# RWKV mixer: the decay's and the rate's narrow projections placed between the key tiles, the values' lerp and the gate behind them

## The chip, the cores and the metric

The kernel runs on one core of a Trainium2 chip. TensorE (PE in the profile) multiplies matrices into PSUM, VectorE (DVE), ScalarE (ACT) and GpSimd (POOL) do the elementwise work, and SyncE (SP) issues most of the transfers. Each engine takes its instructions strictly in its own order, and waits where one needs something that another engine or a transfer has not delivered. The metric is device time in microseconds for one execution, the median of the runs shown. Lower is better.

## The reference

Two layers over 512 latent and 256 context tokens of width 1024. Layer 0 is attention with a feed-forward network, layer 1 is bidirectional RWKV-7 time mixing with a feed-forward network; a last norm gives the output. The change lies in the branches of the time mixer:

```python
def _rwkv_branches(u, mix, w_rkv, w0, w1, w2, a0, a1, a2, g1, g2, k_k, k_a, readout):
    xx = _centred_shift_delta(u)          # 0.5 * (left + right neighbour) - u

    def lerp(j):
        return u + xx * mix[j]

    sel = (0, 2, 3) if readout else (2, 3)
    proj = jnp.einsum('jbtd,jde->jbte', jnp.stack([lerp(s) for s in sel]), w_rkv[-len(sel):])
    k = proj[-2].astype(jnp.float32)
    kk = heads(k * k_k)
    kk = kk * lax.rsqrt(jnp.maximum(jnp.sum(kk * kk, axis=-1, keepdims=True), 1e-24))
    xw, xa = lerp(1), lerp(4)
    for d in range(2):
        w_log = -jax.nn.softplus(-(w0[d] + jnp.tanh(xw @ w1[d]) @ w2[d])) - 0.5
        decay = jnp.exp(-jnp.exp(w_log))
        a = jax.nn.sigmoid(a0[d] + (xa @ a1[d]) @ a2[d])
        k_d = k * (1.0 + (a - 1.0) * k_a)
    r = heads(proj[0])
    g = (jax.nn.sigmoid(lerp(5) @ g1) @ g2)
    return r, heads(proj[-1]), kk, dirs, g
```

So there are six lerps of the same input u and its shift xx. Three feed wide projections (1024 to 1024: r, keys, values), three feed narrow ones (1024 to 128: the decay's w1 of both directions, the rate's a1 of both directions, the gate's g1). A scan over the tokens per direction then uses all of them.

## The kernel before

Activations lie feature-major: 8 tiles (index k or f) of 128 features by 768 tokens (512 for what only the latent tokens need). Every product is made of three matmuls in a reduced 32-bit format: high part times high part, high times low, low times high. A cast on ACT gives the high part of a tile, a subtraction on DVE or POOL the low part. So each lerp tile costs a multiply-add on DVE (`lt`, L911), a cast on ACT (`lh`, L913) and a subtraction (`ll`, L915) of which two in three go to POOL and the others to DVE; each block of weights costs casts on ACT (L218) and subtractions on DVE (L219).

The order in program text of the stage is this. Layer 0 ends with feed-forward products (L445), whose sums are added to xT (L258); both streams are then normed (L521, L522). `dense` (L921) makes the keys: the shift on POOL (L886), the keys' lerp (in its first form, per stream), four weight blocks of 256 columns, two key tiles each; `sink_k` (L948) copies the sums to `kt` (L950) and stores them, squares them (L953) and sums the squares by head on PE (L955, `ssk`). A loop (L972) then makes the decay (w1), the gate (g1) and the rate (a1): a lerp of all eight tiles, its weights, 24 or 48 matmuls. The root of the keys' norm follows (L994 to L1005, `rsy`, `rn`), then the eight normed keys (L1006 to L1014): load `kt`, spread the norm over the features on PE (L1011), multiply (`kkt`, L1013), store. Then come the values' lerp (L1015) and r's lerp (L1018), which is stored to memory and projected later (`project_r`, PE `pr`, L1357).

Behind that scope come the values' products (PE `pv`, L1239 to L1241, 576 matmuls of 256 columns), the elementwise tiles of the scan (`elem`; its first products are `z`, L1073), the triangular inversion on DVE (`invert`, L1169 to L1193), and the scan.

The scheduler orders the instructions of each engine; the text and the pools decide what it may do. Two rules of the pools matter. Tiles with one tag in one pool share a fixed number of buffers, so a new tile waits for the last reader of an older one; lerps share `lt` (two buffers) and a ring of 13 slots for `lh` and `ll`, eight in pool `lp` and five in `lp2`. And pools are stacked from both ends of the memory, so a pool opened later uses the room of one that has been closed and waits for its last readers. On the right stand `lp`, then `lp2`, then the weights' pool `wpj`; when their scope ends, the values open a weights' pool of their own behind `lp`. The scan's tiles (`Xs`, L1040 and others) lie in the room of xT, xx and the other tiles of the key stage on the left.

Of the kernel before, what the change touches and what calls it, by code (L numbers as in the profile page):

```python
# [10 lines left out]
F32 = mybir.dt.float32  # L11
# [26 lines left out]
def tile_hybrid_backbone(ctx: ExitStack, tc: tile.TileContext, a: dict, out: bass.AP, dbg=None, stop=None, start=None):  # L38
# [812 lines left out]
    with ExitStack() as rw:  # L851
# [9 lines left out]
        with ExitStack() as de:  # L861
            lp2 = pool(de, "lp2", side="right")
            wp = pool(de, "wpj", side="right")
# [14 lines left out]
            pk = pool(de, "pk", 1, psum=True)  # L878

# [8 lines left out]
            slots = {"n": 0, "l": 0}  # L888
# [32 lines left out]
            def dense(j, row, n, sink, first=False):  # L921
                xh, xl = lerp(j, n, first=first)
                for b in range(4):
# [7 lines left out]
                    for q in range(2):  # L931
                        if not (first and b == 0):
                            products(items[q:q + 1], xh, xl, KT)
                        out_ = sink(2 * b + q, ps[q][1])
                    if first and b == 0:
# [12 lines left out]
            def sink_k(f, ps):  # L948
                t = ep.tile([P, T], F32, name="kt", tag="kt")
                nc.vector.tensor_copy(t, ps)  # L950
# [7 lines left out]
            dense(2, 1, T, sink_k, True)  # L958
# [13 lines left out]
            for j, nm_, n, dst, fn in ((1, "rwkv_w1", T, t1, AF.Tanh), (5, "rwkv_g1", L, None, AF.Sigmoid),  # L972
                                       (4, "rwkv_a1", T, ta, AF.Copy)):
                xh, xl = lerp(j, n)
                wh, wl = (wp.tile([P, KT, P], F32R, name=z, tag="wd" + z[1], bufs=2) for z in ("wh", "wl"))
                for k0 in range(0, KT, 4):
                    raw = wp.tile([P, 4, P], F32, name="wraw", tag="wdr", bufs=2)
                    if nm_ == "rwkv_g1":
                        nc.sync.dma_start(out=raw, in_=a[nm_][0].rearrange("(k p) f -> p k f", p=P)[:, k0:k0 + 4])
                    else:  # L980
                        for d in range(2):
                            nc.sync.dma_start(out=raw[:, :, 64 * d:64 * d + 64],
                                              in_=a[nm_][0, d].rearrange("(k p) f -> p k f", p=P)[:, k0:k0 + 4])
                    nc.scalar.copy(wh[:, k0:k0 + 4], raw)
                    nc.vector.tensor_tensor(out=wl[:, k0:k0 + 4], in0=raw, in1=wh[:, k0:k0 + 4], op=ALU.subtract)
                outs, full = proj_psum(n)
                product(outs, lambda k: wh[:, k, :], lambda k: wl[:, k, :], xh, xl, KT)
# [530 lines left out]
```

## Time and profile before

| | us |
|---|---|
| median of 3 runs | 2232.61 (2231.56 to 2236.65) |
| profiled execution | 2237.59 |
| its span | 2235.8 |

Busy time of the engines over the span, as the page gives it:

| engine | busy us | share |
|---|---|---|
| PE (matmul) | 2006.4 | 90% |
| DVE | 1636.2 | 73% |
| ACT | 1136.6 | 51% |
| POOL | 693.1 | 31% |

The profile is of one execution. A row of the timeline has the start, the time, the engine, the line, the operation, what it writes and reads, and, in brackets, how long the engine stood idle before it and what ended that. A row of groups has the count, the busy time, the mean of one in ns, and the idle time before them. A row of windows has the length of the stretch, then for PE, PE's weight loads, DVE, ACT and POOL the busy time and the count, then the mean granted clock of PE, the share of the DMA engines and the rate.

### The profile page before, as it was taken

What the parts mean: (1) busy time and instruction counts of PE and PEld (TensorE: products, weight loads), DVE (VectorE), ACT (ScalarE), POOL (GpSimd) and SP (SyncE); (2) the same over time, 40 slices, a digit from 0 to 9 for tenths busy, and PEclk for the clock granted to TensorE, in tenths of its full rate; (3) what the DMA queues carried; (4) which work ended last, traced back from release to release, by engine and by line L of the source; (5) the groups of instructions that cost most, each with busy time, mean ns of one, the idle gap of its engine ahead of it and who ended that gap; (6) DMA issues with size and microseconds to landing.
All of it is one profiled execution on the core that took longest, in us unless ns stands there. A gap on an engine that the chain in (4) does not pass through costs nothing.

```text
span 2235.8 us, 43048 instructions
## 1 busy us (share of the span) xinstructions
PE 2006.4 (90%) x16566; PEld 1770.4 (79%) x16566; DVE 1636.2 (73%) x3105; ACT 1136.6 (51%) x2326; POOL 693.1 (31%) x572
## 2 busy tenths in 40 slices
PE   6998999898999999996988978776988687999998
PEld 4995555697999999995867956665777586899998
DVE  4565555768777777767565598699575778999997
ACT  6436556655333333336343765766665556444443
POOL 1120000126445444423132231221110416666661
PEclk8999999998999999997988989887889888999999
DMA  7206663353221222221336674774645654333332
GB/s 269 99 16 226 227 228 111 122 162 132 76 76 57 76 64 78 66 62 62 102 107 201 181 215 144 216 207 133 188 120 166 185 156 139 117 105 95 104 97 74
DMA packets 249708, 294.12 MB, mean 132 GB/s; under 512 B 36216, under 2 KB 176736, under 8 KB 248992
## 3 DMA queue, kind: packets, MB, share of 16 engines
q1 hardware_dynamic: 248144, 288.42, 41.6%
q8 instruction: 131, 2.15, 0.4%
q0 software_dynamic: 1008, 2.36, 0.3%
q10 hardware_dynamic: 352, 0.60, 0.1%
q14 instruction: 73, 0.60, 0.1%
HBM read 228.40 MB, written 50.33 MB: 125 GB/s over the span
## 4 chain that ended last, share of the span: by engine, by line
PE 65%; DVE 14%; DMA 7%; ACT 6%; issue 5%; POOL 3%; SPq 1%; DVEq 0%; POOLq 0%; ACTq 0%
PE yps L445 12%; PE A L395 8%; PE C L395 5%; PE B L395 5%; PE yps L228 5%; PE po L786 3%; PE pj L228 3%; PE S L767 2%; PE PTp L781 2%; PE mps L126 2%; PE qps L634 2%; PE qps L636 2%; PE qps L635 2%; DVE wu L241 2%; DMA wr<-in_ffn_wu_dram 2%
## 5 line engine op out<-in xcount | busy, mean ns | idle before, releaser
L445 PE MATMUL yps<-gh,wu 128*128 128x384 f32 (+2 forms) x1120 | 323.6, 344 | 0.2 <-DVE xT L258 0.2
L258 DVE SCALAR_TENSOR_TENSOR xT<-yps,modT,xT 128x384 f32<-128x384 f32 (+3 forms) x360 | 185.3, 537 | 119.7 <-PE yps L445 102.1
L239 ACT CAST wu<-wr 128x512 fp32r<-128x512 f32 x276 | 168.5, 619 | 170.6 <-PE A L395 56.4
L239 ACT CAST wu<-ws 128x512 fp32r<-128x512 f32 x176 | 109.2, 621 | 223.8 <-PE yps L445 65.9
L445 PEld LDWEIGHTS yps<-gh,wu 128*128 128x128 f32 x1120 | 202.6, 189 | 11.6 <-DVE xT L258 0.4
L241 POOL TENSOR_TENSOR wu<-wr,wu 128x512 fp32r<-128x512 f32 x86 | 124.8, 1451 | 232.1 <-ACT wu L239 198.4
L445 PE MATMUL yps<-gl,wu 128*128 128x384 f32 (+2 forms) x560 | 192.5, 344 | 0.0
L349 POOL TENSOR_TENSOR ws<-wr 128x512 f32<-128x512 f32 x88 | 130.2, 1484 | 146.0 <-DMA wr<-in_ffn_wg_dram 68.6
L241 DVE TENSOR_TENSOR wu<-wr,wu 128x512 fp32r<-128x512 f32 x190 | 164.3, 869 | 13.4 <-ACT wu L239 12.9
L241 DVE TENSOR_TENSOR wu<-ws,wu 128x512 fp32r<-128x512 f32 x111 | 137.7, 1241 | 21.9 <-ACT wu L239 21.8
L241 POOL TENSOR_TENSOR wu<-ws,wu 128x512 fp32r<-128x512 f32 x65 | 98.9, 1523 | 64.7 <-ACT wu L239 64.6
L228 PE MATMUL yps<-oTh,wu 128*128 128x384 f32 (+1 forms) x512 | 111.3, 309 | 1.1 <-ACT wu L239 1.0
L445 PEld LDWEIGHTS yps<-gl,wu 128*128 128x128 f32 x560 | 105.9, 189 | 4.3
L770 DVE TENSOR_REDUCE mx<-S 128x1 f32<-128x768 f32 (+1 forms) x96 | 74.7, 778 | 44.9 <-PE S L767 44.3
L1156 POOL TENSOR_SCALAR_AFFINE_SELECT GA<-GA 64x512 f32<-64x512 f32 x48 | 41.1, 857 | 202.6 <-ACT GA L1154 191.9
L395 PE MATMUL C<-x5h,wu 128*128 128x384 f32 (+1 forms) x352 | 86.4, 323 | 14.4 <-ACT x5h L312 12.3
L782 ACT COPY PT<-PTp 128x384 f32<-128x384 f32 (+1 forms) x160 | 69.3, 465 | 53.9 <-PE PTp L781 53.8
L781 PEld LDWEIGHTS PTp<-ident,pr 128*128 128x128 f32 x448 | 50.2, 144 | 50.5 <-issue 23.6
L228 PEld LDWEIGHTS yps<-oTh,wu 128*128 128x128 f32 x512 | 85.3, 188 | 1.9 <-ACT wu L239 1.4
L395 PE MATMUL B<-x2h,wu 128*128 128x384 f32 (+1 forms) x352 | 84.7, 309 | 1.3 <-POOL wu L241 1.2
L395 PE MATMUL A<-x1h,wu 128*128 128x384 f32 (+1 forms) x352 | 82.5, 310 | 3.3 <-POOL wu L241 1.7
L241 POOL TENSOR_TENSOR wu<-mw,wu 128x512 fp32r<-128x512 f32 x2 | 2.9, 1446 | 264.6 <-ACT wu L239 264.6
(411 smaller groups left out, 6328.7 us busy)
## 6 DMA issues: line engine op xcount, KB each, us to landing
mw<-in_mod_w_dram SPq DMA_DIRECT2D x48, 1024.0 KB, 5.4
wr<-in_ffn_wg_dram SPq DMA_DIRECT2D x44, 512.0 KB, 4.0
wr<-in_ffn_wu_dram SPq DMA_DIRECT2D x44, 512.0 KB, 3.9
wr<-in_ffn_wd_dram SPq DMA_DIRECT2D x44, 512.0 KB, 3.9
d_b<-BK SPq DMA_DIRECT2D x24, 512.0 KB, 4.3
Bs<-d_b SPq DMA_DIRECT2D x48, 256.0 KB, 3.7
wraw<-in_rwkv_wrkv_dram SPq DMA_DIRECT2D x32, 256.0 KB, 3.2
wr<-in_rwkv_wo_dram SPq DMA_DIRECT2D x16, 512.0 KB, 4.2
```

Of the source, the lines that this page charges most:

```text
L126: nc.tensor.matmul(ps[32 * g:32 * g + 32, :], sc[:, k, :], w[:, k - nk * i, :], start=(k < 4), stop=(k >= 4))
L228: nc.tensor.matmul(ps, w(k), x(k, sl), start=(k == 0 and i == 0), stop=(k == nk - 1 and i == 2))
L239: nc.scalar.copy(hi, raw)
L241: (nc.gpsimd if lane["n"] % 3 == 0 else nc.vector).tensor_tensor(out=lo, in0=raw, in1=hi, op=ALU.subtract)
L258: nc.vector.scalar_tensor_tensor(out=xT[:, f, t0:t1], in0=ps[:, t0 - sl.start:t1 - sl.start], scalar=modT[:, l, 8 * m + f, s:s + 1], in1=x ...
L349: nc.gpsimd.tensor_tensor(out=t, in0=x, in1=y, op=op)
L395: nc.tensor.matmul(ps, w[:, k], x[:, k], start=(k + j == 0), stop=(k == 3 and j == 2))
L445: nc.tensor.matmul(ps, u[k // 2][w][:, k % 2, fs], gs[k // 2][x][:, k % 2, sl], start=(k + j == 0), stop=(k == nk - 1 and j == 2))
L770: nc.vector.tensor_reduce(out=mx, in_=S[:, :nk * P], axis=AX.X, op=ALU.max)
L781: nc.tensor.transpose(ps[:, t - t0, :], pr_[:, P * t:P * t + P], ident)
L782: nc.scalar.copy(PT[h][:, t0:t1, P * qt:P * qt + P], ps[:, :t1 - t0, :])
L786: nc.tensor.matmul(po[HD * h:HD * h + HD, :], vt[:, k0 // P + t, HD * kv:HD * kv + HD], PT[h][:, t, :], start=(t == 0), stop=(t == nk - 1))
```

## The change

Five things change, all in the key stage.

1. The weights' pool `wpj` is opened ahead of `lp2`, so it stands directly behind `lp` and the ring's five slots lie further in. The values' own weights' pool, opened later behind `lp`, then has the place of the old one.
2. The decay and the rate become generators (`low_rank`) with their own weight tiles (`wl_p`), their own PSUM tile of two banks (`pl`), and lerp tiles from the five slots of `lp2`. `dense` calls them behind a key tile: one half of the decay (four of the eight lerp tiles and their 24 matmuls) behind the fourth key tile and one behind the sixth, and the halves of the rate behind the seventh and the eighth.
3. `kt` is copied by ACT instead of DVE.
4. The root of the norm, two normed keys, the values' lerp, six normed keys, the gate, r's lerp: that is the order behind the keys. The gate was ahead of the rate and of the norm.
5. The loop that made the three narrow projections is gone.

```diff
         with ExitStack() as de:
+            wp = pool(de, "wpj", side="right")
             lp2 = pool(de, "lp2", side="right")
-            wp = pool(de, "wpj", side="right")
...
             pk = pool(de, "pk", 1, psum=True)
+            pl = pool(de, "pl", 1, psum=True)
+            wl_p = pool(de, "wlr")
...
                         out_ = sink(2 * b + q, ps[q][1])
+                        if between:
+                            between(b, q)
...
-                nc.vector.tensor_copy(t, ps)
+                nc.scalar.copy(t, ps)
...
+            def low_rank(j, nm_, n, dst, fn, runs):
+                wh, wl = (wl_p.tile([P, KT, P], F32R, name=z, tag=z) for z in ("wh", "wl"))
+                for k0 in range(0, KT, 4):
+                    raw = wp.tile([P, 4, P], F32, name="wraw", tag="wdr", bufs=2)
...
+                    nc.scalar.copy(wh[:, k0:k0 + 4], raw)
+                    nc.vector.tensor_tensor(out=wl[:, k0:k0 + 4], in0=raw, in1=wh[:, k0:k0 + 4], op=ALU.subtract)
+                ps = pl.tile([P, 1024], F32, name="lr", tag="lr")
+                outs = [(ps[:, off:off + w], slice(off, off + w)) for _, off, w in STREAMS if off < n]
+                for run in runs:
+                    for k in run:
+                        hi, lo = (lp2.tile([P, n], F32R, name=z, tag=f"{z}{8 + slots['r'] % 5}") for z in ("lh", "ll"))
+                        slots["r"] += 1
+                        lerp_part(j, k, hi, lo, slice(0, n))
+                        for i, (w, x) in enumerate(((wh, hi), (wh, lo), (wl, hi))):
+                            for o, sl in outs:
+                                nc.tensor.matmul(o, w[:, k], x[:, sl], start=(k == 0 and i == 0), stop=(k == KT - 1 and i == 2))
+                    if run[-1] < KT - 1:
+                        yield
+                if dst is None:
+                    dst = ep.tile([P, T], F32, name="tg", tag="kt")[:, :n]
+                    nc.scalar.activation(dst, ps[:, :n], fn)
+                    nc.sync.dma_start(out=d_g, in_=dst)
+                else:
+                    nc.scalar.activation(dst, ps[:, :n], fn)
+
+            two = [range(0, 4), range(4, KT)]
+            factors = {(1, 1): low_rank(1, "rwkv_w1", T, t1, AF.Tanh, two), (3, 0): low_rank(4, "rwkv_a1", T, ta, AF.Copy, two)}
+            factors[2, 1], factors[3, 1] = factors[1, 1], factors[3, 0]
+            dense(2, 1, T, sink_k, True, lambda b, q: next(factors.get((b, q), iter(())), None))
...
-            for j, nm_, n, dst, fn in ((1, "rwkv_w1", T, t1, AF.Tanh), (5, "rwkv_g1", L, None, AF.Sigmoid),
-                                       (4, "rwkv_a1", T, ta, AF.Copy)):
-                xh, xl = lerp(j, n)
...
-            for f in range(KT):
+            def normed_keys(f):
...
+            for f in range(2):
+                normed_keys(f)
             vxh, vxl = lerp(3, T, lp)
+            for f in range(2, KT):
+                normed_keys(f)
+            for _ in low_rank(5, "rwkv_g1", L, None, AF.Sigmoid, [range(KT)]):
+                pass
```

The scheduler turns this into new orders. In the changed kernel line numbers behind L877 are higher by 2 to 23; names say what is what. Three places follow.

First, DVE at the end of layer 0, where xT takes the last feed-forward sums (`yps`) and the squares of the norm are summed (`acc`). Before, no weight block of the keys is split there:

```order
L241 TENSOR_TENSOR wu<-wr,wu 128x512
L385 TENSOR_TENSOR gl<-gt,gh 128x384
L258 SCALAR_TENSOR_TENSOR xT<-yps,modT,xT 128x256 x3
L178 TENSOR_TENSOR acc<-acc,sq 128x256 x2
L258 SCALAR_TENSOR_TENSOR xT<-yps,modT,xT 128x256
L178 TENSOR_TENSOR acc<-acc,sq 128x256
L258 SCALAR_TENSOR_TENSOR xT<-yps,modT,xT 128x512
```

The same place in the changed kernel:

```order
L241 TENSOR_TENSOR wu<-wr,wu 128x512
L385 TENSOR_TENSOR gl<-gt,gh 128x384
L219 TENSOR_TENSOR wlo<-wraw,whi 128x512
L258 SCALAR_TENSOR_TENSOR xT<-yps,modT,xT 128x256
L219 TENSOR_TENSOR wlo<-wraw,whi 128x512
L258 SCALAR_TENSOR_TENSOR xT<-yps,modT,xT 128x256 x2
L178 TENSOR_TENSOR acc<-acc,sq 128x256
L258 SCALAR_TENSOR_TENSOR xT<-yps,modT,xT 128x256
L178 TENSOR_TENSOR acc<-acc,sq 128x256
L219 TENSOR_TENSOR wlo<-wraw,whi 128x512
```

All eight subtractions of the first two blocks (`wlo`), with their casts on ACT, now stand among these; before, they stood between the norm and the keys' lerp.

Second, PE behind the fourth key tile. Its last products and, behind them, what is new (`lr` is the narrow projection's sum; the rows go on like this to 24):

```order
L228 MATMUL pj<-lh,wlo 128x512
L228 MATMUL pj<-lh,wlo 128x256
L984 MATMUL lr<-lh,wh 128x512
L984 MATMUL lr<-lh,wh 128x256
L984 MATMUL lr<-ll,wh 128x512
L984 MATMUL lr<-ll,wh 128x256
L984 MATMUL lr<-lh,wl 128x512
L984 MATMUL lr<-lh,wl 128x256
```

Before, the next key tile's products followed there, and the decay's products came behind all keys. There are four such pieces now, and the values' products begin behind the last normed key as before. Of these, 238 stood ahead of the first z before, and 153 stand there now; between the first z and the end of the fourth elementwise tile there are nearly as many as before (317 and 313), and behind that tile 110 instead of 21.

Third, DVE between the keys and the values' products. Before, these are lerps of the rate, the first of the values, and normed keys (`kkt`):

```order
L1013 SCALAR_TENSOR_TENSOR kkt<-kt,hkk,pj 128x768
L911 SCALAR_TENSOR_TENSOR lt<-xx,par_78,xT 128x768 x2
L1013 SCALAR_TENSOR_TENSOR kkt<-kt,hkk,pj 128x768
L915 TENSOR_TENSOR ll<-lt,lh 128x768
L911 SCALAR_TENSOR_TENSOR lt<-xx,par_78,xT 128x768 x2
L1013 SCALAR_TENSOR_TENSOR kkt<-kt,hkk,pj 128x768 x2
L911 SCALAR_TENSOR_TENSOR lt<-xx,par_78,xT 128x768
L219 TENSOR_TENSOR wlo<-wraw,whi 128x512 x2
L911 SCALAR_TENSOR_TENSOR lt<-xx,par_78,xT 128x768
```

In the changed kernel the values' lerps are over at this place, and between the normed keys stand the last lerps of the gate (512 wide) and r's (L1041, which is L1018 before):

```order
L1030 SCALAR_TENSOR_TENSOR kkt<-kt,hkk,pj 128x768
L913 SCALAR_TENSOR_TENSOR lt<-xx,par_78,xT 128x512
L917 TENSOR_TENSOR ll<-lt,lh 128x512
L913 SCALAR_TENSOR_TENSOR lt<-xx,par_78,xT 128x512 x2
L1030 SCALAR_TENSOR_TENSOR kkt<-kt,hkk,pj 128x768
L1041 SCALAR_TENSOR_TENSOR lt<-xx,par_78,xT 128x512
L917 TENSOR_TENSOR ll<-lt,lh 128x512
L1030 SCALAR_TENSOR_TENSOR kkt<-kt,hkk,pj 128x768
L1041 SCALAR_TENSOR_TENSOR lt<-xx,par_78,xT 128x512
L1030 SCALAR_TENSOR_TENSOR kkt<-kt,hkk,pj 128x768
```

The weights of the values' first two blocks (eight `wlo`) are split ahead of the third normed key; before, the first of them stood behind the last.

More of the change, by code (lines that the diff above doesn't have):

```diff
@@ L886, in shift @@
                 nc.gpsimd.tensor_tensor(out=y[:, 1:w - 1], in0=x[:, 0:w - 2], in1=x[:, 2:w], op=ALU.add)
-            slots = {"n": 0, "l": 0}
+            slots = {"n": 0, "l": 0, "r": 0}
             def lerp(j, n, own=None, first=False):
@@ L919, in proj_psum, with dense @@
                 return [(ps[:, off:off + w], slice(off, off + w)) for _, off, w in STREAMS if off < n], ps[:, :n]
-            def dense(j, row, n, sink, first=False):
+            def dense(j, row, n, sink, first=False, between=None):
                 xh, xl = lerp(j, n, first=first)
@@ L956, in sink_k @@
                 return t
-            dense(2, 1, T, sink_k, True)
+            def low_rank(j, nm_, n, dst, fn, runs):
+                wh, wl = (wl_p.tile([P, KT, P], F32R, name=z, tag=z) for z in ("wh", "wl"))
+                for k0 in range(0, KT, 4):
+                    raw = wp.tile([P, 4, P], F32, name="wraw", tag="wdr", bufs=2)
+                    if nm_ == "rwkv_g1":
+                        nc.sync.dma_start(out=raw, in_=a[nm_][0].rearrange("(k p) f -> p k f", p=P)[:, k0:k0 + 4])
+                    else:
+                        for d in range(2):
+                            nc.sync.dma_start(out=raw[:, :, 64 * d:64 * d + 64],
+                                              in_=a[nm_][0, d].rearrange("(k p) f -> p k f", p=P)[:, k0:k0 + 4])
+                    nc.scalar.copy(wh[:, k0:k0 + 4], raw)
[16 more added lines that the diff above has]
+                    nc.sync.dma_start(out=d_g, in_=dst)
+                else:
+                    nc.scalar.activation(dst, ps[:, :n], fn)
@@ L971, in tile_hybrid_backbone @@
             nc.vector.tensor_copy(hsel, ps)
-            for j, nm_, n, dst, fn in ((1, "rwkv_w1", T, t1, AF.Tanh), (5, "rwkv_g1", L, None, AF.Sigmoid),
-                                       (4, "rwkv_a1", T, ta, AF.Copy)):
-                xh, xl = lerp(j, n)
[L975 to L987, printed above, removed]
-                if dst is None:
-                    dst = ep.tile([P, T], F32, name="tg", tag="kt")[:, :n]
-                    nc.scalar.activation(dst, full, fn)
-                    nc.sync.dma_start(out=d_g, in_=dst)
-                else:
-                    nc.scalar.activation(dst, full, fn)
             sm_, y_, t_ = (nm.tile([P, 6 * NH], F32, name=z) for z in ("ssm", "rsy", "rst"))
```

## The prediction

> **What bounds the kernel now.** I read the page first, for the span and the chain that ended last.
>
> ```profile
> span 2235.8 us, 43048 instructions
> PE 65%; DVE 14%; DMA 7%; ACT 6%; issue 5%; POOL 3%; SPq 1%; DVEq 0%; POOLq 0%; ACTq 0%
> ```
>
> PE (TensorE) has two thirds of the chain, but that is a mean over many stages. So I cut the stretch that the change touches, the key part of the RWKV mixer and what follows it, into windows at events named below: from the end of layer 0 to the first key tiles, the other six key tiles, the narrow projections and the normed keys, the values up to the first decay product (`z`), and two more up to the end of the projection of r.
>
> ```profile
> core 0: us, PE busy (x) PEld busy (x) DVE busy (x) ACT busy (x) POOL busy (x), PEclk, DMA share, GB/s
> 1023.00:1070.00 47.00, 27.91 (x124) 23.51 (x123) 39.83 (x66) 32.27 (x63) 17.62 (x26) 0.71 0.16 55
> 1070.00:1132.00 62.00, 60.15 (x375) 53.59 (x374) 30.64 (x36) 18.08 (x25) 9.26 (x5) 1.00 0.32 103
> 1132.00:1184.00 52.00, 41.61 (x165) 29.52 (x164) 44.30 (x47) 23.91 (x34) 21.88 (x14) 0.78 0.50 158
> 1184.00:1222.00 38.00, 32.94 (x239) 31.73 (x240) 23.24 (x27) 13.37 (x25) 10.13 (x9) 0.90 0.60 197
> 1222.00:1281.00 59.00, 58.82 (x504) 56.78 (x503) 28.06 (x50) 39.80 (x94) 11.96 (x19) 0.97 0.60 166
> 1281.00:1384.00 103.00, 84.89 (x742) 64.97 (x743) 95.10 (x210) 59.35 (x135) 27.11 (x32) 0.90 0.64 187
> ```
>
> The second row is PE's alone: 60.2 of 62 us, at a granted clock of 1.00, with DVE (VectorE) half idle and POOL (GpSimd) almost so. The third is the reverse: DVE 44.3 of 52 us, PE at clock 0.78. The fifth is PE's again, the last DVE's (95.1 of 103). The change shifts work from the third window into the second. The timeline has the events:
>
> ```profile
> 1042.81 0.79 PE L228 MATMUL pj<-lh,whi 128*128 128x256 f32 x2 [8.40 <-ACT lh L913]
> 1132.30 1.04 PE L970 MATMUL hps<-ident,hb 128*48 128x128 f32 x8
> 1184.55 1.01 PE L1239 MATMUL pv<-whi,lh 128*128 128x256 f32 x3 [3.71 <-ACT whi L218]
> 1186.78 0.58 PE L1240 MATMUL pv<-wlo,lh 128*128 128x256 f32 x1 [1.22 <-DVE wlo L219]
> 1213.20 1.82 POOL L1040 MEMSET Xs<- 128x2048 f32 x1 [18.44 <-DVE lt L1018]
> 1221.73 0.67 PE L1073 MATMUL z<-t,wa 128*128 128x256 f32 x2 [3.05 <-DMA wa<-in_rwkv_w_dram]
> 1280.70 1.99 DVE L1169 STREAM_TRANSPOSE E<-AB 128x1024 f32<-128x1024 f32 x1 [4.41 <-ACT AB L1161]
> 1281.06 0.28 PE L1240 MATMUL pv<-wlo,lh 128*128 128x256 f32 x1
> 1281.18 0.28 PE L1241 MATMUL pv<-whi,ll 128*128 128x256 f32 x1
> 1298.06 0.79 PE L1357 MATMUL pr<-rh,whi 128*128 128x512 f32 x1 [0.26 <-ACT whi L218]
> 1383.48 0.39 PE L1357 MATMUL pr<-rh,wlo 128*128 128x512 f32 x1
> ```
>
> Keys end at 1132.3, values (`pv`) run from 1184.6 to 1281.3, the first z stands at 1221.7 because its tiles overlay xx and xT, which L1018 on DVE reads last. The triangular inversion starts at 1280.7.
>
> **Part 1, weights ahead of the norm.** Of the first two weight blocks, eight casts on ACT and eight subtractions on DVE move into the tail of layer 0, as the first pair of order listings shows.
>
> ```profile
> L219 DVE TENSOR_TENSOR wlo<-wraw,whi 128x512 fp32r<-128x512 f32 x8 | 6.0, 752 | 1.0 <-ACT whi L218 0.8
> L218 ACT CAST whi<-wraw 128x512 fp32r<-128x512 f32 x8 | 4.9, 612 | 3.4 <-DMA wraw<-in_rwkv_wrkv_dram 3.4
> 1043.72 0.69 DVE L219 TENSOR_TENSOR wlo<-wraw,whi 128x512 fp32r<-128x512 f32 x1 [0.17 <-ACT whi L218]
> 1044.73 0.69 DVE L219 TENSOR_TENSOR wlo<-wraw,whi 128x512 fp32r<-128x512 f32 x1
> ```
>
> Not all 6.0 us lie on the path. I count one subtraction ahead of the norm's second half (0.7), the two inside the lerps (1.4), and two casts between the modulations (1.2): **3.3 us** earlier for the first key tiles. The ends are 0 (the region is no earlier free) and 6.0. Its cover is layer 0's tail, where PE is full and DVE waits for PE; without cover the same 6.0 come back there. Two subtractions of the decay's own factor take the place of two that left before the norm's second half; I don't count them.
>
> **Part 2, decay and rate among the keys.** On PE nothing is added or taken away; 96 matmuls move.
>
> ```profile
> 1100.45 8.44 PE pj L228 x48
> 1108.89 1.23 PE ssk L955 x12
> ```
>
> ```profile
> L911 DVE SCALAR_TENSOR_TENSOR lt<-xx,par,xT 128x768 f32<-128x768 f32 x12 | 15.2, 1286 | 1.7 <-POOL ll L915 1.7
> L1013 DVE SCALAR_TENSOR_TENSOR kkt<-kt,hkk,pj 128x768 f32<-128x768 f32 x8 | 8.1, 1011 | 2.9 <-DMA kt<-d_k 1.7 <-PE pj L1011 1.1
> L915 POOL TENSOR_TENSOR ll<-lt,lh 128x768 fp32r<-128x768 f32 x8 | 15.2, 1907 | 17.4 <-ACT lh L913 17.4
> ```
>
> The first two rows are the chain of waits within the second window, the others groups of the third, each with its count, busy time, mean in ns and idle time before it. One key tile is 48 matmuls in 8.44 us, so each half of a narrow projection (24 of the same shapes) is 4.2 us. Three halves stand ahead of the last key tile's end, one behind it. Keys then end at 1132.3 - 3.3 + 12.7 = **1141.7**, PE full as now. That needs sixteen lerps in time, each 1.3 us of DVE and for two in three 1.9 of POOL, where that window has 31 and 53 us idle; a late one makes PE wait in order, 1.9 us at each of four places. I take none. The copy of `kt` goes from DVE to ACT: eight at no more than the 1.0 of a kkt, which reads PSUM too, beside PE on either engine (ACT has 44 us idle there). If a tile's sums came free too late for the next but one, PE would wait that 1.0 at each; I take nothing.
>
> **Part 3, what is left behind the keys.** Now values' lerps, gate and normed keys stand between the keys and the values' products, and DVE does them in order (third pair of listings). Its prices, with the window's own contention in them, are those groups and these:
>
> ```profile
> L911 DVE SCALAR_TENSOR_TENSOR lt<-xx,par,xT 128x512 f32<-128x512 f32 x8 | 7.9, 998 | 0.0
> L915 DVE TENSOR_TENSOR ll<-lt,lh 128x768 fp32r<-128x768 f32 x5 | 5.3, 1068 | 0.0
> L985 DVE TENSOR_TENSOR wl<-wraw,wh 128x512 fp32r<-128x512 f32 x4 | 2.7, 684 | 0.2 <-ACT wh L984 0.2
> L915 DVE TENSOR_TENSOR ll<-lt,lh 128x512 fp32r<-128x512 f32 x2 | 1.7, 853 | 0.0
> L915 POOL TENSOR_TENSOR ll<-lt,lh 128x512 fp32r<-128x512 f32 x6 | 8.0, 1344 | 14.2 <-ACT lh L913 14.2
> L1000 DVE SCALAR_TENSOR_TENSOR rsy<-rst,rsy 128x96 f32<-128x96 f32 x1 | 1.3, 1282 | 0.0
> L971 DVE CAST hsel<-hps 48x1024 fp32r<-48x1024 f32 x1 | 1.2, 1209 | 0.0
> 1159.41 1.82 POOL L915 TENSOR_TENSOR ll<-lt,lh 128x768 fp32r<-128x768 f32 x1 [0.52 <-ACT lh L913]
> 1159.61 2.43 DVE L911 SCALAR_TENSOR_TENSOR lt<-xx,par,xT 128x768 f32<-128x768 f32 x1
> 1163.01 1.01 DVE L911 SCALAR_TENSOR_TENSOR lt<-xx,par,xT 128x768 f32<-128x768 f32 x1
> ```
>
> The last key product needs a PSUM slot that the sixth `kkt` frees, and values follow it in PE's order. Up to that `kkt` DVE has: seven of the values' lerps 9.0 (their slots come free with the last key tile), two of their subtractions 2.1, eight gate lerps 8.0 and three subtractions 2.6, six kkt 6.1, ten weight subtractions 6.8 (two of the gate's factor, eight of the values' blocks, which used to come behind), hsel and rsy 2.5, and five short ones on the way to the norm with the first r lerp, for which I estimate 3.5 at the 0.7 of a weight subtraction. Sum 40.6. The idle time in it is bounded below by none, above by the 7.7 that stands before DVE now (52.0 - 44.3). Without contention (1.01 instead of 1.286, and as much off the narrower ones) it is 4 us less. So 37 to 48; I take **42**, near the rows' own sum: little of the idle time stays, as the first two key tiles are loaded early. (On SP's queue eight loads of values' weights now stand ahead of the third; if it comes late, that is the 1.7 of kkt's row, within the 7.7.) Values' products start at 1141.7 + 42 = **1183.7**, against 1184.6: almost all that was won is spent behind the keys, since DVE's work there is as long as before, only with other contents. Two more waits are new: the first values' PSUM bank is that of the gate's sum, so PE also waits for the sigmoid behind a table load on ACT; with the last gate product ahead of the last kkt this is covered, uncovered it is the load and the sigmoid, of which I have no row here and which I bound by the 3.7 that pv waits for ACT now. PE's clock is low in the block either way (0.78 now), so values start slowly as they do now.
>
> **Part 4, behind the start of the values.** Here the order gains more.
>
> ```profile
> L1018 DVE SCALAR_TENSOR_TENSOR lt<-xx,par,xT 128x512 f32<-128x512 f32 x8 | 5.9, 747 | 4.3 <-DMA d_rl<-lt 4.3
> ```
>
> The lerps are done, both first weight blocks loaded (3.7 and 1.2 us of waits in the rows above go, of which the start already holds the first), and L1018's eight reads of xx stand directly behind the normed keys. The first z follows 153 values' products instead of 238. At 0.12 us each (the two rows at 1281) that is 10.2 us less, with 1.2 + 3.1 of waits gone: 1183.7 + 37.2 - 10.2 - 4.3 = 1206.4, that is **15.3 earlier**. Its tiles allow it if the last read of xx is over by about 1197.9 (now 8.5 us lie between them): two kkt and seven reads fill 7.3 us behind the start, with the 4.3 that they wait for transfers 11.6: at 1195.3 they are over. The inversion starts 15.3 earlier too, as PE's order between z and it holds the same work. But the 85 products come behind z: values end at 1281.3 - 15.3 + 10.2, **5.1 earlier**. The projection of r can't start before that (its tiles lie where the values' lerps lay), and the next elementwise tiles live where r's lay. So the gain at 1383.5 lies between 5.1 (r follows the values) and 15.3 (DVE full, all of its lead kept). I take **8**, nearer to the first, as PE has 85 of 103 us there. Behind it nothing is changed and I carry the 8 us through.
>
> **Sum.** The profiled execution took 2237.59 us, its span 2235.8; it would take 2229.6. The median shown, 2232.61, lies 5 below that execution; less the same 8 us it gives **2224.6**.
>
> **Rivals.**
> *All of DVE's lead is kept*: r's projection is fed sooner as well, and the 18 us in which PE is idle after 1281 shrink. For it: DVE 92% busy there. Against: r's start. Gain 15 to 16, 2217.
> *Spent twice*: the block behind the keys takes 48 instead of 42. Values start at 1189.7 and end at 1282.2, so r is 1 later, the inversion 9 earlier: 2232, no change.
> *The port, slower*: while POOL subtracts, DVE's lerp took 2.43 instead of 1.01 (the two rows above; POOL's began at 1159.41). Ten such subtractions now fall into the block, five at 1.9 and five at 1.3, 16.3 us. If DVE stood for all of each, on 37 + 7.7, the block takes 61, values start 18 later and end 13 later: 2246. It decides from a block of 47 us on, where the values' end is no longer earlier. Against it: now fourteen such operations cost about 5 us, not 23.2.
> The Trainium skill, SBUF — State Buffer, "Who interferes with whom", says that a DVE instruction with two SBUF inputs and a GpSimd instruction that reads SBUF exclude each other for the whole instruction. By that rule the time would be this rival's; the trace agrees in the row of 2.43 us, and disagrees in its mean of 1.286 us.
> *Not what it says*: the weights' region is free no earlier, and part 1 is 0: 2228.
>
> **How the numbers follow.** Forecast 0.40, all kept 0.22, spent twice 0.18, port 0.12, region 0.08. What a measurement can tell from no change is about 0.2%, 4.5 us. Faster: 0.36 of the forecast, 0.22, 0.02 and 0.05 of the others, 0.65. Same: 0.04, 0.13 and 0.03, 0.20. Slower: 0.15. The range reaches to the first rival and past no change, with the block at 37 to 48 in it (6 us each way): 2213 to 2236; the port lies outside.
>
> **What would show it.** Part 1: the first pj after layer 0 about 2 us earlier, no weight casts between the modulations. Part 2: PE full between the key tiles, `hps` at about 1146. Part 3: first pv at 1178 to 1190, DVE over 85% busy before it. Part 4: first z at 1206, values' end at 1276, inversion at 1265, r's end at 1375. I am wrong if PE waits for `ll` among the keys, if pv starts before 1175 or after 1190, or if r's end doesn't move though the inversion does.

## The result: 0.7% slower, and the profile after

| | us |
|---|---|
| changed kernel, median of 13 runs | 2253.55 (2247.23 to 2258.35) |
| kernel before, median of 13 runs beside them | 2236.72 (2231.56 to 2251.51) |
| ratio, 95% interval | 1.0068 (1.0054 to 1.0082) |
| profiled execution, its span | 2256.64, 2254.9 |

By the ratio that is about 15 us more, where 8 less were forecast. The page's first line and its chain of waits read much as they did:

```profile
span 2254.9 us, 43054 instructions
PE 65%; DVE 14%; DMA 8%; ACT 5%; issue 4%; POOL 3%; SPq 1%; DVEq 0%; POOLq 0%; ACTq 0%
```

So the difference has to be looked for at events. First the clock of the comparison must be set right. The last product of layer 0, in the timeline of before and then of after:

```profile
1022.94 0.40 PE L445 MATMUL yps<-gh,wu 128*128 128x512 f32 x1
```

```profile
1027.96 0.40 PE L445 MATMUL yps<-gh,wu 128*128 128x512 f32 x1
1045.59 0.58 PE L228 MATMUL pj<-lh,whi 128*128 128x256 f32 x1 [6.96 <-ACT lh L915]
1147.96 0.51 PE L228 MATMUL pj<-lh,whi 128*128 128x512 f32 x2
1167.69 0.37 PE L1020 MATMUL rnp<-ident,rsy 128*16 128x128 f32 x1 [12.24 <-DVE rsy L1017]
1200.01 0.58 PE L1262 MATMUL pv<-whi,lh 128*128 128x256 f32 x1 [5.25 <-ACT tg L989]
1220.39 0.38 PE L1096 MATMUL z<-t,wa 128*128 128x256 f32 x1
1279.08 2.04 DVE L1192 STREAM_TRANSPOSE E<-AB 128x1024 f32<-128x1024 f32 x1 [4.41 <-ACT AB L1184]
1290.24 0.28 PE L1264 MATMUL pv<-whi,ll 128*128 128x256 f32 x1
1357.30 2.03 DVE L1192 STREAM_TRANSPOSE E<-AB 128x1024 f32<-128x1024 f32 x1 [2.33 <-ACT AB L1184]
1396.64 0.39 PE L1380 MATMUL pr<-rh,wlo 128*128 128x512 f32 x1
```

The 5.0 us at layer 0's end are not shown to be the change's: PE's order is the same in both kernels up to the third key tile, over the fourteen executions profiled for this study that product stands anywhere from 1019.8 to 1028.0, and e9 below, in which PE, DVE, ACT and POOL have the changed kernel's order up to there and far beyond, reaches it at 1022.8. So all that follows is counted in us behind it. The inversions are numbered from (0) in order of time. "Last key product" is the last one of two high parts (`lh,whi`); four more, 0.7 us, end the keys.

| event | before | forecast | after |
|---|---|---|---|
| first key product | 19.9 | 16.6 | 17.6 |
| last key product | 108.5 | 117.9 | 120.2 |
| first product of the values | 161.6 | 160.8 | 172.0 |
| first z | 198.8 | 183.5 | 192.4 |
| inversion (0) | 257.8 | 242.5 | 251.1 |
| last product of the values | 258.2 | 253.1 | 262.3 |
| inversion (1) | 319.8 | | 329.3 |
| last product of r | 360.5 | 352.5 | 368.7 |
| scan over (first product of the output) | 783.3 | 775.3 | 796.9 |
| end | 1212.9 | 1204.9 | 1227.0 |

Up to the keys the forecast holds within 2.3 us. Then 9 more are lost at one place, ahead of the values, which start 11.2 us late. Windows from the last key product to the first of the values, from there to the last, and to the last of r, before and after (columns as in the prediction's windows):

```profile
1131.80:1184.55 52.75, 41.81 (x167) 29.69 (x165) 44.85 (x48) 24.63 (x35) 22.43 (x14) 0.78 0.50 160
1184.55:1281.35 96.80, 92.10 (x745) 88.86 (x746) 51.10 (x76) 52.65 (x118) 21.66 (x28) 0.94 0.60 178
1281.35:1384.00 102.65, 84.54 (x739) 64.62 (x740) 94.75 (x210) 59.35 (x135) 26.99 (x31) 0.90 0.64 187
```

```profile
1103.00:1148.40 45.40, 45.40 (x281) 40.58 (x280) 22.58 (x19) 16.55 (x22) 15.20 (x12) 1.00 0.23 71
1148.40:1200.01 51.61, 27.60 (x96) 16.77 (x94) 41.57 (x46) 22.57 (x33) 17.94 (x10) 0.61 0.57 190
1200.01:1290.50 90.49, 88.82 (x745) 86.47 (x746) 44.96 (x84) 45.58 (x107) 19.44 (x27) 0.98 0.57 167
1290.50:1397.00 106.50, 91.77 (x823) 69.54 (x821) 88.50 (x190) 63.45 (x142) 24.57 (x28) 0.89 0.64 187
```

The block behind the keys is as long as it was (51.6 against 52.75), but PE now does 14.2 us less in it. The work that left it was put where PE was full (45.40 of 45.40), so it made the keys longer by as much; and in the block nothing took its place. What PE waits for in the block after the change, then DVE and ACT:

```profile
PE rnp L1020 <- DVE rsy L1017: 12.2, 1, 12.2
PE pv L1262 <- ACT tg L989: 5.2, 1, 5.2
PE pj L1028 <- DVE rn L1022: 3.1, 1, 3.1
...
DVE lt L913 <- POOL ll L917: 4.1, 2, 3.0
DVE kkt L1030 <- DMA kt<-d_k: 3.9, 2, 2.4
DVE wl L974 <- ACT wh L973: 1.6, 1, 1.6
...
ACT L989 <- DVE kkt L1030: 6.6, 1, 6.6
```

12.2 us go by while the norm's root is made on DVE: there the narrow projections used to stand. Then the values wait for the gate's sigmoid (`tg`), because their first bank is that of its sum. And the sigmoid waits for a `kkt`, though the gate's sum is done:

```profile
1192.88 1.00 DVE L1030 SCALAR_TENSOR_TENSOR kkt<-kt,hkk,pj 128x768 f32<-128x768 f32 x1
1193.35 0.39 PE L984 MATMUL lr<-lh,wl 128*128 128x512 f32 x1
1196.98 1.01 DVE L1030 SCALAR_TENSOR_TENSOR kkt<-kt,hkk,pj 128x768 f32<-128x768 f32 x1 [2.44 <-DMA kt<-d_k]
1198.06 1.28 ACT L989 ACT_TABLE_LOAD   x1 [6.59 <-DVE kkt L1030]
1199.36 0.60 ACT L989 ACTIVATE tg<-lr 128x512 f32<-128x512 f32 x1
```

The first row is the sixth `kkt`, the third the seventh. The gate's last product is out by 1193.74. But `tg` is written into one of the two slots of `kt`; that slot is read by the seventh `kkt`, which waits 2.44 us for its load. So a transfer of the keys holds up the values, by way of a slot, the sigmoid and a bank.

### The profile page after: what moved, and what is told of

Read it like the earlier page. It is cut to its first block, busy times and chain, and to the rows that moved or that the text cites. A ratio compares the mean times of both kernels' runs of the same rounds, so it can differ in the third digit from the quotient of the medians.

```text
span 2254.9 us, 43054 instructions
## 1 busy us (share of the span) xinstructions
PE 2012.4 (89%) x16566; PEld 1772.3 (79%) x16566; DVE 1630.6 (72%) x3097; ACT 1144.2 (51%) x2335; POOL 696.0 (31%) x572
## 4 chain that ended last, share of the span: by engine, by line
PE 65%; DVE 14%; DMA 8%; ACT 5%; issue 4%; POOL 3%; SPq 1%; DVEq 0%; POOLq 0%; ACTq 0%
PE yps L445 12%; PE A L395 8%; PE B L395 5%; PE C L395 5%; PE yps L228 5%; PE pj L228 3%; PE po L786 3%; PE S L767 2%; PE PTp L781 2%; PE pr L1380 2%; PE mps L126 2%; PE qps L634 2%; PE qps L636 2%; PE qps L635 2%; POOL ws L349 2%
## 5 line engine op out<-in xcount | busy, mean ns | idle before, releaser
L349 POOL TENSOR_TENSOR ws<-wr 128x512 f32<-128x512 f32 x88 | 130.9, 1493 | 144.1 <-DMA wr<-in_ffn_wg_dram 72.1
L241 DVE TENSOR_TENSOR wu<-wr,wu 128x512 fp32r<-128x512 f32 x190 | 160.5, 850 | 13.2 <-ACT wu L239 12.6
L241 DVE TENSOR_TENSOR wu<-ws,wu 128x512 fp32r<-128x512 f32 x111 | 138.8, 1251 | 20.6 <-ACT wu L239 20.4
```

The costliest lines, as they stand in the source:

```text
L241: (nc.gpsimd if lane["n"] % 3 == 0 else nc.vector).tensor_tensor(out=lo, in0=raw, in1=hi, op=ALU.subtract)
L349: nc.gpsimd.tensor_tensor(out=t, in0=x, in1=y, op=op)
```

## The experiments

All are edits of the changed kernel. The table has what the traces show, in us behind layer 0's last product: the first and last product of the values, PE's idle time from the last key product to the last of the values (length less busy time in the windows view), inversion (1), the last product of r, and the time from inversion (1) to the scan's end; then the ratio to the kernel before. The ratio is of all runs, the rest of one execution each. The runs of one edit spread over 4 to 15 us, so a few us between two rows prove little where they lie far from the edit.

| kernel | values from | to | PE idle | inv. (1) | r to | inv. (1) to scan's end | ratio (95%) |
|---|---|---|---|---|---|---|---|
| before | 161.6 | 258.2 | 15.6 | 319.8 | 360.5 | 463.4 | 1 |
| changed | 172.0 | 262.3 | 25.7 | 329.3 | 368.7 | 467.6 | 1.0068 (1.0054 to 1.0082) |
| e1 | 171.3 | 262.7 | 26.8 | 332.2 | 370.2 | 451.5 | 1.0018 (0.9999 to 1.0037) |
| e2 | 144.1 | 244.4 | 9.7 | 303.2 | 360.7 | 450.7 | 0.9849 (0.9822 to 0.9875) |
| e3 | 172.6 | 263.5 | 25.4 | 331.8 | 371.2 | 457.3 | 1.0031 (1.0014 to 1.0047) |
| e4 | 183.0 | 270.9 | 33.4 | 338.7 | 378.3 | 453.0 | 1.0033 (1.0016 to 1.0050) |
| e5 | 131.7 | 258.4 | 23.9 | 322.4 | 360.2 | 459.8 | 1.0027 (1.0012 to 1.0043) |
| e6 | 140.3 | 237.1 | 4.6 | 307.2 | 347.6 | 459.0 | 0.9945 (0.9928 to 0.9961) |
| e7 | 178.8 | 268.2 | 24.4 | 335.5 | 374.9 | 453.9 | 1.0045 (1.0028 to 1.0062) |
| e8 | 141.6 | 227.1 | 4.3 | 305.9 | 349.2 | 464.5 | 0.9988 (0.9972 to 1.0004) |
| e9 | 165.9 | 255.1 | 19.9 | 319.7 | 362.9 | 471.9 | 1.0043 (1.0023 to 1.0062) |
| e10 | 158.6 | 250.6 | 17.5 | 313.9 | 353.1 | 445.6 | 0.9954 (0.9939 to 0.9970) |
| e11 | 141.9 | 243.8 | 10.5 | 299.5 | 356.4 | 467.7 | 0.9985 (0.9969 to 1.0002) |
| e12 | 138.5 | 239.7 | 10.5 | 296.6 | 359.0 | 470.8 | 0.9943 (0.9925 to 0.9960) |

**e1_hb_early.** The lines from `hbf = ...` to the copy into `hsel` move ahead of `dense(2, ...)`.

> The changed kernel, but the head pattern hb and its transposes (hps, hsel) are built ahead of the keys' lerp, so that hb does not hold one of the two lt slots while the last lerps of the rate and the first of the values are made. In the changed kernel's profile values' products start 172.1 us behind the last product of layer 0 (161.6 before), and DVE is idle for 8.4 us between 1144 and 1153.7. Theory A (the slot): the lerps no longer go one by one there, values start at 164 to 168 and the time falls by 4 to 8 us against the changed kernel, to 1.003 to 1.005 of the kernel before. Theory B (the gate): values' products wait for the gate's sigmoid, which waits for the seventh kkt and the load of its kt; then DVE's lead is not used, values start at 170 to 172 and the time stays at 1.006 to 1.008. Either way the scheduler puts 103 instead of 153 values' products ahead of the first z.

Values start at 171.3: theory B, the slot is not what holds them (PE still waits 4.1 us for the sigmoid). Yet the time falls, and further than theory A said, to 1.0018. The table shows where: not up to r's end, which is 1.5 us later than in the changed kernel, but in the scan, which is 16 us shorter. Neither theory had that.

**e2_gate_first.**

```diff
+            for _ in low_rank(5, "rwkv_g1", L, None, AF.Sigmoid, [range(KT)]):
+                pass
             for f in range(2):
                 normed_keys(f)
```

> The changed kernel, but the gate's narrow projection stands between the root of the norm and the first two normed keys, instead of behind the last normed key. Theory B (the gate): in the changed kernel PE is idle for 5.3 us ahead of the values' products, until the sigmoid behind a table load is over; here that wait goes, values start 165 to 168 us behind layer 0's last product instead of 172.1. Theory C (DVE's sum): DVE does the same work ahead of the last kkt, so values start at 170 to 172. The scheduler puts 294 instead of 153 values' products ahead of the first z, so this also tells what the end follows: if the projection of r and the scan follow the end of the values' products, the time falls to 1.002 to 1.005 of the kernel before; if they follow the inversion, which is then 10 to 12 us later, it rises to 1.010 to 1.013.

Far more than either theory: values start 28 us earlier, since they now run between the normed keys. PE's waits from the last key product to the end of the values, the two longest:

```profile
PE pj L1028 <- DVE kkt L1030: 2.4, 2, 2.1
PE lr L984 <- ACT lh L915: 1.3, 2, 0.8
```

The root's wait, 12.2 us before, is 0.4 here, as the gate's products stand in it. The values end 17.9 us earlier and inversion (1) comes 26 us earlier, but r only 8.0; another 17 us are gained from inversion (1) to the scan's end. This version is faster than both kernels.

**e3_undo_pool.** The two lines that open `wpj` and `lp2` change places again.

> The changed kernel with the two pools of part 1 in their old order, so the keys' first weights are split behind layer 0 again. Theory (part 1 does what was said): the first key product stands 19 to 20 us behind layer 0's last product (17.6 in the changed kernel, 19.9 before), and the time rises by 1 to 4 us against the changed kernel, to 1.007 to 1.009 of the kernel before. Rival (part 1 costs: its casts and subtractions delay the tail of layer 0, or the values' weights now wait for the region): the time falls below 1.005, and the first key product's distance does not grow.

The first key product stands at 20.0, 2.4 us later: part 1 does what it says, though by the start of the values 0.6 of it is left. Up to r's end the kernel is 2.5 us slower, as expected; the time is the rival's (below 1.005) all the same, with a scan that is 10 us shorter.

**e4_no_between.** `dense` gets no `between`; `low_rank(1, ...)` and `low_rank(4, ...)` run whole behind the copy into `hsel`.

> The changed kernel, but the decay's and the rate's narrow projections are not placed between the key tiles: they follow the keys in program text, with the same pools, lerp slots and order of the rest. Theory (the interleave gains what it says, DVE bounds the block behind the keys): keys end 12.7 us earlier, and some 16 lerps and 5 subtractions (26 us of DVE) come back into the block, so values start 180 to 190 us behind layer 0's last product (172.1) and the time is 1.010 to 1.014 of the kernel before. Rival (the interleave costs: late lerps stop PE among the keys, and PE has nothing left to cover the norm's root with, 12.2 us idle in the changed kernel): values start at 165 to 172, and the time is at or below the changed kernel's 1.007.

Keys end at 107.6, 12.6 us earlier, and values start at 183.0, 11 later: the theory's mechanism and size. The interleave by itself is worth some 9 us at inversion (1): DVE's lerps go under the keys as well, so the stretch from the last key product to the values, 75.4 us here, shrinks to 51.8. What costs is then the rest of the change, and e2 points to the gate's place behind the normed keys: against the kernel before, e4's values start 21 us later, and the interleave wins back half of that. The time hides it and is the rival's (1.0033): the scan is 14.6 us shorter.

**e5_gate_pd.**

```diff
-                ps = pl.tile([P, 1024], F32, name="lr", tag="lr")
+                ps = pd.tile([P, 1024], F32, name="lr", tag="pj") if dst is None else pl.tile([P, 1024], F32, name="lr", tag="lr")
```

> The changed kernel in its own order of the text (gate behind the last normed key), but the gate's sum is a tile of the pool pd that the normed keys use, not of pl. The first values' bank is then freed by the copy of the rate's sum, 127 us behind layer 0's last product, not by the gate's sigmoid. Theory B (the bank): values' products start at 128 to 145 us instead of 172.0 and run beside the normed keys, the values end 10 to 20 us earlier than in the changed kernel, and the time falls to 0.983 to 0.997 of the kernel before. Rival (the run with the gate ahead of the normed keys was faster for its order on DVE, or for the order that the scan got): values start early here too or not, but the time stays above 1.000.

The bank is what held the start: it falls to 131.7. But the values end only 3.9 us earlier. Now 72 of their products stand ahead of the normed keys, and all the others behind them and the gate, so PE waits between the normed keys instead:

```profile
PE pj L1028 <- DVE kkt L1030: 12.2, 6, 3.2
PE pv L1262 <- ACT whi L218: 4.5, 1, 4.5
PE lr L984 <- DVE kkt L1030: 2.2, 1, 2.2
```

PE's idle time is nearly what it was (23.9). So not when the values start decides, but how much of them stands in PE's gaps.

**e6_gate_between** and **e8_hb_gate_between.** The gate's generator goes into `factors` at (0, 1), in e8 with e1's edit as well. The gate's lerp there reads xx before its last step (the factor 0.5 and the subtraction of u, behind the first two key tiles), so these two kernels compute the gate from other numbers; the work is the same.

> The changed kernel, with the gate's narrow projection among the key tiles as well (all of it behind the second). Theory B: the sigmoid is over long before the values, so they start at 125 to 140 us behind layer 0's last product, and DVE's work behind the keys is less by the gate's eight lerps and its subtractions, about 10 us; the last read of xx (183.9 in the changed kernel, 184.4 with the gate first) comes at 172 to 178, the inversion at 235 to 245, and the time is 0.975 to 0.984 of the kernel before. Rival (DVE and POOL can't feed eight more lerps under the keys): the keys' last product comes 5 us or more later than 120.2 + 2.8, and the time is no better than with the gate first (0.985).

> The changed kernel with the gate among the key tiles and the head pattern hb built ahead of the keys. With the wait for the gate gone, theory A (the slot that hb holds) can show: the values' lerps start up to 8 us earlier, the last read of xx comes 2 to 8 us earlier than with the gate among the keys alone, and the time falls by 2 to 6 us against it, 0.972 to 0.983 of the kernel before. Rival: the ring's subtractions on POOL limit the lerps, not the slot: no difference beyond 0.2%.

Both signs of e6's rival came: the last key product stands at 133.2, and the time, 0.9945, is no better than e2's. Of the 13.0 us, 3.0 are there at the first key product, and the gate's 24 products of 512 columns take 5.5 at 0.23 each (the expectation's 2.8 was half of that); the other 4.5 are mostly PE's waits for the square on ACT (4.0). Still PE is idle for only 4.6 us behind them, and r ends 21 us earlier than in the changed kernel. Inversion (0) comes at 264.3, though, not at 235 to 245. In e8 the last read of xx comes at 163.6 instead of 181.8, more than expected, but 413 values' products stand ahead of the first z, which comes at 200.4: nothing uses the lead, and the time is 0.4% above e6's, as neither of e8's theories had it.

**e7_kt_dve.** `nc.vector.tensor_copy(t, ps)` again in `sink_k`.

> The changed kernel with the copy of kt back on DVE (eight copies of about 0.96 us among the keys). The prediction put this edit at nothing: DVE waits there anyway, the start of the values is held by the gate, and the order on PE is nearly the same; so 1.005 to 1.0085 of the kernel before. Rival: the copy delays the lerps of the decay and the rate, which then stop PE among the keys, by up to 7.7 us: 1.009 to 1.011.

The rival's size, by a wait of another name: the last key product comes 7.1 us later, as PE doesn't stop for a lerp but once for the square on ACT, which reads the same sum and stands behind a lerp's cast there. r ends 6.2 us later.

```profile
PE ssk L959 <- ACT kq L957: 5.4, 1, 5.4
```

The time, 1.0045, is lower than the changed kernel's even so and below both forecasts, with a scan that is 13.7 us shorter.

**e9_tg_own.** `dst` of the gate becomes a tile of `lp2` with the tag of the next free `lh` slot.

> The changed kernel, but the sigmoid writes the gate (tg) into a free lerp slot of lp2, not into a slot of kt. PE's order is the same as in the changed kernel up to the first z, ahead of which now stand 203 values' products instead of 153. Theory B in detail: in the changed kernel the sigmoid was late because its output waited for the slot of kt that the seventh kkt reads, and that kkt for the load of its kt; the last gate product was over long before. Then values' products start at 166 to 169 us behind layer 0's last product instead of 172.0, right behind the last product of the normed keys, values end 3 to 8 us earlier than at 262.3, and the time falls to 1.000 to 1.005 of the kernel before. Rival (the last gate product or the table load is late by itself): 171 to 172, and 1.005 to 1.008.

```profile
1186.78 1.28 ACT L989 ACT_TABLE_LOAD   x1 [3.01 <-PE lr L984]
1188.07 0.60 ACT L989 ACTIVATE tg<-lr 128x512 f32<-128x512 f32 x1
1188.72 0.58 PE L1262 MATMUL pv<-whi,lh 128*128 128x256 f32 x1 [1.09 <-ACT tg L989]
```

The sigmoid now follows the gate's products, and PE waits 1.09 us for it instead of 5.25. Values start 6.1 us earlier, end 7.2 and r 5.8 earlier, as expected. But 2.7 us of each lie ahead of the last key product, where the order on PE, DVE, ACT and POOL is the same; so the slot is worth some 3.4 at the start of the values.

**e10_hb_tg_own, e11_gate_31, e12_hb_gate.** e10 is e9 with e1's edit; e11 has the gate directly behind `dense`; e12 is e2 with e1's edit.

> The kernel with tg in a lerp slot, and the head pattern hb built ahead of the keys. The gate's lerps then come early enough that the scheduler puts 70 values' products between the normed keys. Theories A and B together: values start at 150 to 163 us behind layer 0's last product, the last read of xx comes at 172 to 178 (175.5 with hb early alone), values end at 248 to 256, and the time is 0.988 to 0.999 of the kernel before. Rival (the start of the values does not carry to the end, the scan's order decides): the time stays at 1.000 to 1.004 though values end earlier.

> The changed kernel with the gate's narrow projection directly behind the last key tile, ahead of hb and the norm's root: much the order of the run with the gate ahead of the normed keys (0.985), made by another place in the text, so that the scan gets another order. If that run's gain comes from the values' products that run beside the normed keys: values start at 140 to 148 us behind layer 0's last product and end at 242 to 248, and the time is 0.980 to 0.990 of the kernel before. If half of it or more was the order that the scan got there (r's projection ended no earlier than before, 360.7 against 360.5 us, but the scan 29 us earlier): the same start, and 0.990 to 1.000.

> The changed kernel with the gate ahead of the first normed keys and hb built ahead of the keys. Theory A, now that values don't wait for the gate: DVE gets to the values' and the gate's lerps earlier, values start at 136 to 142 us behind layer 0's last product (144.1 with the gate first alone), the last read of xx comes at 172 to 182 (184.4), and the time is 2 to 8 us less than with the gate first alone, 0.981 to 0.984 of the kernel before. Rival: the lerps wait for POOL and the ring rather than for hb's slot, or the scan's order outweighs it: 0.985 to 0.998.

In all three the values start where expected, and in e10 and e11 they end so; in e12 they end 5 us earlier than in e2. In e10 the last read of xx comes at 181.2, not at 172 to 178. e10's time, 0.9954, is as forecast; e11's is that of its second case, and e12's that of its rival. These two part ways with e2 behind the edit: they reach inversion (1) 4 and 7 us ahead of it and are slower by 1.4% and 0.9%, with 17 us more to the scan's end in e11 and 20 in e12. Against the changed kernel they keep 0.8% and 1.3% of e2's 2.2%. So about half of e2's gain comes from behind the edit, most likely from the order that its scan got; no run shows that order by itself.

**The scan.** From inversion (1) to the scan's end the fourteen kernels take 445.6 to 471.9 us. Their work there is not quite the same, since more or less of r's projection lies ahead of it. But kernels with nearly equal counts differ as much: the changed kernel and e1 have about 5670 instructions on PE and 735 on DVE there and take 467.6 and 451.5; e2 and e12 have about 5980 and 760 and take 450.7 and 470.8. That they differ in order is seen on DVE from inversion (3) to (4), where `Sn` ends a scan step. After the change, five steps stand ahead of the inversion; these are the last two, with it:

```profile
1602.86 0.68 DVE L1344 TENSOR_TENSOR Sn<-pn,S 128x512 f32<-128x512 f32 x1
1622.63 0.68 DVE L1344 TENSOR_TENSOR Sn<-pn,S 128x512 f32<-128x512 f32 x1
1623.23 1.95 DVE L1192 STREAM_TRANSPOSE E<-AB 128x1024 f32<-128x1024 f32 x1
```

In e1, as in the kernel before, it comes behind the fourth:

```profile
1595.02 0.67 DVE L1344 TENSOR_TENSOR Sn<-pn,S 128x512 f32<-128x512 f32 x1
1602.62 1.96 DVE L1192 STREAM_TRANSPOSE E<-AB 128x1024 f32<-128x1024 f32 x1
```

From inversion (3) to (4) it is 114.4 us after, 102.4 before and 97.6 in e1. This one place doesn't explain the times: e4 also has five steps there and takes 453.0 to the scan's end, e11 has four and takes 467.7. Why the scheduler put it so wasn't found, and no run held the scan's order fixed.

## Why the prediction failed, step by step

**Part 1** was right in kind and 1 us too large: 2.3 instead of 3.3, and e3 takes 2.4 back.

**Part 2** was right for PE: full between the key tiles, the keys longer by 14.0 without part 1's gain, where 12.7 were forecast. Of these 14.0, about 2.5 arise in the third key tile, ahead of every product that was moved (see the last section). The copy of `kt` hides on ACT as said. But its worth was mis-sized: left on DVE it would have cost 7.1 us (e7), not nothing.

**Part 3 is the step that failed**: the sigmoid, of which it says "with the last gate product ahead of the last kkt this is covered". From the keys' end to the end of the sixth `kkt`, over which the prediction summed DVE's work, the window is this:

```profile
1149.00:1193.88 44.88, 26.17 (x90) 15.95 (x88) 39.23 (x44) 20.09 (x31) 17.94 (x10) 0.62 0.52 172
```

DVE is busy for 39.2 us, where the sum was 40.6, and idle for 5.7, where 7.7 was the bound. So the sum was right, and "I take 42, near the rows' own sum: little of the idle time stays" was 2.9 too small, within the stated 37 to 48. But the values don't follow the sixth `kkt`. PE does the last normed keys' products and then waits 5.25 us for the sigmoid, a wait that was put at nothing, or at 3.7 if uncovered. The last gate product does stand ahead of the last `kkt`, but the sigmoid doesn't follow that product: it waits for a slot that the sum of the gate has nothing to do with, for the seventh `kkt` and for its load. That chain was not looked for. The load of the table and the sigmoid are 1.9 of the 5.25; the prediction had "no row here" for them, but the profile before has:

```profile
1154.38 1.28 ACT L990 ACT_TABLE_LOAD   x1
1155.67 0.60 ACT L990 ACTIVATE tg<-pj 128x512 f32<-128x512 f32 x1
```

So the values start 11.2 late, by some 2.3 at the keys' end, 2.9 up to the sixth `kkt` and 6.1 behind it. Behind this lies a plainer omission. The 12.7 us of products were rightly added to the keys, but what PE would do in the block that they left wasn't asked: it is busy there for 27.6 of 51.6 us. e2, e11 and e12 put values' products there: PE's idle time falls from 25.7 to about 10 us, and values end 18 to 23 us earlier.

**Part 4** had the order's arithmetic right. The first z came 20.4 behind the values' start (22.7 forecast), and the values' end lost 10.5 against z (10.2 forecast). So with the late start z gained only 6.4 us, and the values' end came 4.1 later. What failed is the bracket for r: it was to gain between the values' end (5.1) and the inversion (15.3), but r's end came 8.2 later, outside on the far side of the values' end. The lead of inversion (0) was worth nothing, since it was gone one inversion later: inversion (1) follows the first values' product by 158.2 us before and by 157.3 after, and by 153.8 to 160.9 in all the other kernels but e5, e6 and e8, whether 103 values' products stand ahead of the first z (e1) or 294 (e2). From the values' end on, PE has 91.8 us of work up to r's end instead of 84.5, and DVE, which was to set the pace, is idle for 18.0 us (106.50 - 88.50) instead of 7.9. In e9 too, values end 3.1 earlier than before and r ends 2.4 later.

**"Behind it nothing is changed"** was wrong as well: the scan's order changed. Of the 14.1 us by which the changed kernel ends later, 9.5 are there at inversion (1), and 4.2 come behind it, up to the scan's end. The 9.5 are the 10.4 by which the values start later than before, less 0.9. The 4.2 are less than the 16 to 20 us by which kernels with nearly equal counts differ there; their cause stays open.

**The rivals.** The block came out above the 47 us from which the port's rival decides, and the sign was that rival's. Its mechanism was not: the 61 us had DVE busy for 53.3 of them (37 and 16.3), and it is busy for 41.57. Its price per operation can be seen:

```profile
1161.30 3.19 POOL L917 TENSOR_TENSOR ll<-lt,lh 128x768 fp32r<-128x768 f32 x1 [6.38 <-ACT lh L915]
1161.82 1.00 DVE L913 SCALAR_TENSOR_TENSOR lt<-xx,par,xT 128x768 f32<-128x768 f32 x1
1164.45 1.81 POOL L917 TENSOR_TENSOR ll<-lt,lh 128x768 fp32r<-128x768 f32 x1
1164.53 2.55 DVE L913 SCALAR_TENSOR_TENSOR lt<-xx,par,xT 128x768 f32<-128x768 f32 x1
```

Beside the first subtraction the lerp takes its usual 1.00 us and the subtraction 3.19; beside the second, which takes 1.81, the lerp takes 2.55. So the price falls now on one engine and now on the other. The rule cited there from the Trainium skill (SBUF — State Buffer, "Who interferes with whom"), that the two exclude each other for a whole instruction, is compatible with both; what the rival had wrong is that DVE pays each time. The nearest rival was "spent twice", with its block of 48: the same place, a smaller price, and no wait named that would make it so.

## What to carry to other kernels

Work that is moved from where an engine idles to where it is full buys nothing on that engine (here PE; the move paid by DVE's share of it); name what will stand in the hole, and what that needs: its operands, its bank, its slot. A wait in front of a new tile is not over when the last user of the memory could be done, so follow that user back through its own output's slot to the transfer at the end of the chain. Where one scheduler orders the whole program, a local edit reorders stages hundreds of us later, here with differences larger than the edit's own; judge it at events in the trace next to the edit, and the total only over several versions.

## What was not expected of the hardware

- With less work in the block, PE's granted clock there is lower: 0.61 instead of 0.78. With more products standing directly behind each other afterwards it is 0.98 instead of 0.94, and 745 PE instructions take 88.8 us instead of 92.1.
- The same order doesn't take the same time. With one PE order up to there, layer 0 ends within 8.1 us over fourteen executions; and from there to the last key product the changed kernel takes 120.2 and e9 117.5, with one order on PE, DVE, ACT and POOL. The difference arises at the third key tile: PE is busy throughout in both, for 12.4 us at a granted clock of 0.77 and for 9.7 us at 1.00. Both have a gap of 1.3 us shortly before it; behind it the clock falls to 0.50 for 6.8 us (1074.70 to 1081.50) in the changed kernel and stays at 1.00 in e9. Why it differs stays open.
- The sigmoid starts 0.02 us behind its table load of 1.28 us. The load ahead of the norm's root starts 0.02 us behind the cast before it (at 1157.88) and has the root 0.02 us behind its end; no further cost of the switch shows in this trace.
